# adaLN weight segments held in fours, and eight row tiles of products issued back to back

## The chip, the core and the metric

The kernel runs on one core of a Trainium2 chip. The metric is the device time of one execution in microseconds (us); lower is better. The engines that matter here are TensorE (PE in the profile, with its weight loads as PEld), VectorE (DVE), ScalarE (ACT), GpSimd (POOL) and the SyncE queue (SP), which issues nearly all weight transfers.

## The reference

One decoder layer is applied to a prompt of 256 rows and to eight samples of eight rows, 320 rows in all, with D_MODEL = 2048. Everything is float32.

```python
mod = silu(c) @ w_ada + b_ada                     # c: 9 rows, w_ada: 2048 x 12288
sh1, sc1, gt1, sh2, sc2, gt2 = split(mod, 6)
h = rmsnorm(x, g_pre_mix) * (1 + sc1) + sh1
proj = h @ w_in                                   # 2048 x 5136: q k v, z, a, b, u
o  = gated delta rule on conv(q, k, v), 8 heads, gated by silu(z)
y5 = S5 state space on u, gelu, @ w_glu, gate, norm
x = x + gt1 * rmsnorm(concat(o, y5) @ w_out, g_post_mix)
h = rmsnorm(x, g_pre_ffn) * (1 + sc2) + sh2
f = (silu(h @ w_gate) * (h @ w_up)) @ w_down      # 5632 wide
x = x + gt2 * rmsnorm(f, g_post_ffn)
```

The change is about the first line. Its nine rows of `c` (one of the prompt, eight of the samples) meet a weight matrix of 100 MB, nearly a third of all the bytes that the kernel reads.

## The kernel before, in words

**Streamed weights.** Each weight matrix comes through twelve buffers ("slots") of [128, 1024] float32, 512 KB each. A `Seg` is one such piece: `nk` row tiles of 128 rows by `ncol` columns. The list `items` holds all segments in the order in which TensorE uses them. `fetch` issues loads on the SyncE queue, in that order, as long as more than `WRES = 3` slots are free. `pump` splits a loaded segment into a high part (`whi`, a copy on ScalarE, L490) and a low part (`wlo`, a subtraction on VectorE, L491), each in a slot of its own, after which the raw slot is free again. It looks at no segment that lies `AHEAD = 4` or more places beyond the current one, and it wants three free slots. `mm3` then makes three products for every 128 x 128 block of weights, with 320 columns of activations as the moving operand.

**adaLN segments** are not split. They are used as they come, with the weights as the moving operand and the nine rows of `silu(c)`, padded to 32 columns, as the stationary one. A product thus fills 32 of the array's 128 columns. Row tile `kt` goes to column group `kt % 4`, which writes 32 of the 128 partitions of one PSUM bank (`ps_ax`); `ada_tail` copies the bank out (`adaev`), transposes it and adds up the four groups. Twenty-two blocks of 512 columns have eight segments of two row tiles each; two blocks of 384 columns have eight of two, and two of 128 columns have two of eight. A float32 product shows as two matmul instructions in the trace, so a segment of two row tiles is four of them.

**Order of the work.** `merge` interleaves the adaLN segments in proportion with the split segments of the stage: with the input projection (four slabs of 1, 3, 4 and 8 row tiles; blocks for a slab are computed during the slab before it), with the GLU, with the first half of the output projection and with the first of four blocks of the feed-forward. Two blocks stand alone, while the first sub-layer's residual is formed. The other work (convolution, S5, delta rule) is written as generators that run "in the background": after each step of `mm3` and after each segment `tick` lets them emit what an emission clock expects to be ready. All engines' streams are in order, so this clock sets where the background work stands between the streamed products. The clock charges 0.024 us for an adaLN product whose column group is not the first.

Of the kernel before, what the change touches and what calls it, by code (L numbers as in the profile page):

```python
# [79 lines left out]
class Seg:  # L80
    """One streamed [128, <=1024] piece of a weight matrix: kts row tiles by cols columns."""

    def __init__(self, src, k0, nk, c0, nc_, body, split=True):
        self.src, self.k0, self.nk, self.c0, self.ncol = src, k0, nk, c0, nc_
        self.body, self.split = body, split
        self.raw = self.hi = self.lo = None


class Paced:
    """The operations of a layer as generators, which wait until the operands are expected to be there."""  # L90
# [20 lines left out]
class Layer:  # L111
    def __init__(self, ctx, tc, I, O, stop=None):
# [12 lines left out]
        self.stage_end, self.in_bg = 0.0, False  # L125
        nc = self.nc
# [3 lines left out]
    # ---------------------------------------------------------------- emission clock  # L130
    # The instruction streams are in order, so what runs in the background is emitted where its
    # inputs are expected to be there; the clock below estimates when that is, from the engines'
    # queues and the last writes and reads of each tile.
# [15 lines left out]
    def _start(self, eng, outs, ins, same):  # L149
        """When the operands allow an operation of an engine to start."""  # L150
# [15 lines left out]
    def fits(self, eng, outs, ins):  # L166
        """Whether an operation emitted now would hardly hold up its engine."""
        c = self.clk
        t = self._start(eng, outs, ins, 0.0)
        if eng == "PE":  # L170
            return t <= c["now"] + self.EPS_PE
        return (eng == "SP" or c[eng] <= c["now"] + self.LIM) and t <= max(c[eng], c["now"]) + self.EPS
# [28 lines left out]
    def _slot(self, tile, tag, cap):  # L201
        """A new tile takes the place of the one of its tag whose last use lies furthest back."""
# [9 lines left out]
    def ready(self, *aps):  # L212
        """When these are written."""
        return max((self.rd[k][0] for ap in aps for k in self._keys(ap) if k in self.rd), default=0.0)
# [5 lines left out]
    def mbank(self, tag="mm"):  # L220
        """A PSUM bank that has been read when the streamed products get to it."""
# [7 lines left out]
    def gate(self, *ts):  # L229
        """Let the background go on until these times."""  # L230
# [75 lines left out]
    def mm(self, out, lhsT, rhs, start=True, stop=True):  # L306
# [8 lines left out]
        if not self._run("PE", c, (out,), (lhsT, rhs)):  # L315
            return
        return self.T.matmul(out, lhsT, rhs, start=start, stop=stop)  # L317

    def tr(self, out, in_, b=0):
        p = in_.shape[0]  # L320
        if not self._run("PE", 0.00086 * p, (out,), (in_,)):
# [12 lines left out]
    def take(self, tag, n=1):  # L334
        """Wait until n buffers of a tag are free; give() returns them once their last use is emitted."""
# [9 lines left out]
    def idle(self, tag):  # L345
        """PSUM banks of a tag that are free and have been read."""
# [7 lines left out]
    def bg(self, gens, k=1, front=False):  # L354
        """Run generators in the background, k of them at a time; each yield waits for what it emitted."""
# [39 lines left out]
    # ---------------------------------------------------------------- streaming  # L395
# [8 lines left out]
    def emit(self):  # L404
# [5 lines left out]
        for it in self.items:  # L410
# [10 lines left out]
            for t in (it.hi, it.lo) if it.split else (it.raw,):  # L421
                self.wput(t)
            it.raw = it.hi = it.lo = None
            self.cur += 1

    def fetch(self):
        """Load ahead, leaving room for a split and one column block of adaLN."""
# [4 lines left out]
    def pump(self, force=-1):  # L432
        """Split the segments that have arrived, as far ahead as there is room."""
# [12 lines left out]
    def ws(self, name, dt=F32):  # L446
        """The slot that has been free the longest."""
# [15 lines left out]
    def _dma(self, q, n, out=None, in_=None):  # L463
        """A transfer of n words from one of the queues."""
# [28 lines left out]
    def mm3(self, s, ps, m, act, first, last):  # L493
        """ps += W[:, chunk m].T @ act over the row tiles of s; act(kt) -> (hi, lo)."""
# [11 lines left out]
    def split_act(self, hl, src):  # L506
        """hl [128, 2, N] f32r <- hi and lo parts of src [128, N]."""
# [6 lines left out]
    # ---------------------------------------------------------------- phase 0  # L514
    def setup(self):
# [28 lines left out]
        # row vectors, one feature tile per partition: those of the first norm, and the others  # L544
# [33 lines left out]
        # silu(c), transposed, nine rows padded to 32  # L578
# [14 lines left out]
        # mean square of x, and x transposed  # L593
# [10 lines left out]
        # per-feature columns  # L604
# [17 lines left out]
    def setup_x(self):  # L622
        """Eight feature tiles of x, transposed; and the mean squares."""
# [19 lines left out]
    def setup_x2(self):  # L643
        """The other eight."""
# [11 lines left out]
    def setup_late(self):  # L656
        """The other per-feature columns; the space of the inputs goes to the mixer."""
# [25 lines left out]
    def later(self, t):  # L683
        """Hold a background stage back for t more microseconds."""
# [34 lines left out]
    # ---------------------------------------------------------------- adaLN  # L719
    def ada(self, c0, ncol):  # L720
        """Segments that leave mod[:, c0/128 .. , :] for ncol (256 or 512) columns of w_ada."""
        nk = 1024 // ncol
        st = {}

        def body(s):
            if s.k0 == 0:
# [4 lines left out]
            for kk in range(nk):  # L731
                kt = s.k0 + kk
                g = kt % 4
                self.mm(ps[32 * g:32 * g + 32, :ncol], self.cs[:, kt, :],
                        s.raw[:, kk * ncol:(kk + 1) * ncol], start=kt < 4, stop=kt >= KT - 4)
                if g == 3 and kk < nk - 1:
                    self.tick()
# [4 lines left out]
        return [Seg(self.I["w_ada"][0], k0, nk, c0, ncol, body, split=False) for k0 in range(0, KT, nk)]  # L742
# [23 lines left out]
    def modulate(self, kt, rsb, sh0, dst):  # L766
        """hi/lo of (x * rs) * A + shift for one feature tile, in place of x."""
# [36 lines left out]
    # ---------------------------------------------------------------- input projection  # L804
# [141 lines left out]
    def put(self, kind, i, ps, si):  # L946
        """Add a finished chunk to its place."""
# [39 lines left out]
    def z_gate(self, i):  # L987
        """Twice silu(z)."""
# [8 lines left out]
    # ---------------------------------------------------------------- conv  # L997
    def conv_hist(self):
        """Last rows of the conv state, transposed in front of each sample's columns."""
# [15 lines left out]
    def conv_state(self):  # L1015
        """The last rows of every sequence before the convolution, back in rows, four tiles at a time."""
# [50 lines left out]
    def expm1(self, out, x, tmp):  # L1067
        """exp(x) - 1 of a small tile: 2^k * series(x - k ln 2) + (2^k - 1)."""
# [19 lines left out]
    # ---------------------------------------------------------------- S5 tables  # L1088
    def trans(self, nm, src, hf):
        """Four tables from the transposes of src."""  # L1090
# [8 lines left out]
    def c_tables(self):  # L1099
        """Per channel tile, block diagonal over the two groups of a pair: two each of re and im of  # L1100
        [(pair, abar B or B, channel), state], then [state, (pair, channel)] of C and abar C; here C."""
# [23 lines left out]
    def s5_setup(self):  # L1125
# [49 lines left out]
        # angle in turns, reduced to half a turn either way  # L1175
# [10 lines left out]
        # sine and cosine - 1 from series at a quarter of the angle  # L1186
# [99 lines left out]
    # ---------------------------------------------------------------- S5 scan  # L1286
# [15 lines left out]
    def s5_in(self, ch):  # L1302
        """Even and odd steps of a pair's channels on top of each other, two pairs to 128 partitions."""
# [12 lines left out]
    def s5_pair(self, q):  # L1316
        """Two groups: states on the partitions, every second step held, in a rotating frame."""
# [82 lines left out]
    def s5_state_out(self):  # L1400
        """Final states back to rows of (group, state)."""
# [21 lines left out]
    # ---------------------------------------------------------------- gated delta rule  # L1423
# [1092 lines left out]
```

## Time and profile before

| | |
|---|---|
| median of 3 runs | 1903.72 us (1900.76 to 1905.53) |
| span of the profiled execution | 1904.5 us; no other time of that execution is given |
| TensorE busy | 1845.4 us (97%) |
| TensorE weight loads | 1603.9 us (84%) |
| VectorE, ScalarE, GpSimd busy | 1007.1, 771.5, 384.9 us |
| mean granted TensorE clock | 0.987 |
| read from HBM | 321.25 MB |

The span runs from the first to the last instruction. Matmuls are pipelined and their ends are modelled, so that two neighbours overlap in the record; the time that one takes from the others is read from the start of one to the start of the next. DMA share is the mean busy share of the sixteen DMA engines.

### The profile page before, as it was taken

The page shows a single profiled execution, that of the slowest core. Times are in us where ns is not written, and L with a number is a line of the kernel's source. Part 1 is how long each engine was busy: PE and PEld are TensorE (multiplying, and loading weights), DVE is VectorE, ACT ScalarE, POOL GpSimd, SP SyncE. Part 2 cuts the span into 40 slices and gives each one's busy share as a digit, 9 for nine tenths or more (in the row PEclk, how much of TensorE's full clock was granted, in tenths as well). Part 3 has the DMA queues.
Part 4 walks back from the last instruction along what each step waited for, and adds up shares of the span by engine and source line. Part 5 has one row for each costly group of instructions (what it writes and reads, how often), then busy time and mean ns, then how long its engine had stood idle before and what let it go on. Part 6 is the DMA issues. An engine that isn't in the chain of part 4 may idle for free.

```text
span 1904.5 us, 32280 instructions
## 1 busy us (share of the span) xinstructions
PE 1845.4 (97%) x12619; PEld 1603.9 (84%) x12619; DVE 1007.1 (53%) x1896; ACT 771.5 (41%) x1503; POOL 384.9 (20%) x577
## 2 busy tenths in 40 slices
PE   6899999999999989999899999999999999999998
PEld 4667787666677667789699999999999999999997
DVE  3677677878764554543833333444444334434444
ACT  3433355545564434453533333333333333333343
POOL 1003674666404211115600000000000000000043
PEclk9999999999999988999999999999999999999999
DMA  8899644555585964676565556454555545655452
GB/s 267 273 322 292 162 115 143 180 170 172 169 262 152 278 185 117 182 222 209 179 176 158 161 171 184 146 155 132 147 167 154 146 132 149 171 148 151 128 150 89
DMA packets 487953, 336.38 MB, mean 177 GB/s; under 512 B 29328, under 2 KB 439656, under 8 KB 487472
## 3 DMA queue, kind: packets, MB, share of 16 engines
q1 hardware_dynamic: 473842, 328.60, 58.3%
q10 hardware_dynamic: 13542, 5.40, 1.1%
q8 instruction: 99, 1.62, 0.4%
q14 instruction: 54, 0.43, 0.1%
q0 software_dynamic: 416, 0.32, 0.1%
HBM read 321.25 MB, written 13.02 MB: 176 GB/s over the span
## 4 chain that ended last, share of the span: by engine, by line
PE 89%; DVE 4%; DMA 3%; POOL 2%; ACT 1%; issue 1%; SPq 0%; ACTq 0%; DVEq 0%; POOLq 0%
PE ps_mm L317 43%; PE ps_bA L317 22%; PE ps_bB L317 15%; PE ps_ax L317 6%; PE ps_bB L323 1%; POOL tab L279 1%; DVE wlo L491 1%; DVE u L279 1%; PE ps_bA L323 1%; PE ps_mm L323 1%; DVE acc L279 1%; DMA x<-in_x_prompt_dram 1%; DMA braw<-in_b_im_dram 1%; DMA raw<-in_w_in_dram 0%; ACT whi L490 0%
## 5 line engine op out<-in xcount | busy, mean ns | idle before, releaser
L491 DVE TENSOR_TENSOR wlo<-raw,whi 128x1024 fp32r<-128x1024 f32 (+2 forms) x441 | 496.4, 1126 | 612.0 <-ACT whi L490 369.5
L490 ACT ACTIVATE whi<-raw 128x1024 fp32r<-128x1024 f32 (+2 forms) x441 | 424.3, 964 | 398.9 <-DVE wlo L491 289.5
L317 PE MATMUL ps_mm<-h,whi 128*128 128x320 f32 x1344 | 297.0, 308 | 0.0
L317 PE MATMUL ps_mm<-hT,whi 128*128 128x320 f32 x1204 | 289.9, 326 | 6.1 <-DVE hT L279 3.7
L317 PEld LDWEIGHTS ps_mm<-hT,whi 128*128 128x128 f32 x1204 | 198.2, 191 | 54.9 <-issue 32.1
L317 PEld LDWEIGHTS ps_mm<-h,whi 128*128 128x128 f32 x1344 | 224.4, 187 | 4.2 <-ACT gs L262 1.7
L317 PE MATMUL ps_mm<-h,wlo 128*128 128x320 f32 x672 | 206.6, 307 | 0.0
L317 PE MATMUL ps_mm<-hT,wlo 128*128 128x320 f32 x602 | 187.5, 311 | 0.0
L279 POOL TENSOR_TENSOR sqa<-acc 128x320 f32<-128x320 f32 x1 | 0.7, 722 | 863.3 <-DVE acc L279 863.3
L317 PE MATMUL ps_bA<-h,whi 128*128 128x320 f32 x736 | 163.8, 310 | 1.5 <-ACT whi L490 1.5
L317 PE MATMUL ps_bB<-h,whi 128*128 128x320 f32 x736 | 162.7, 308 | 0.0
L317 PE MATMUL ps_mm<-f,whi 128*128 128x320 f32 x704 | 155.7, 309 | 0.0
L317 PE MATMUL ps_ax<-raw,cs 128*32 128x512 f32 (+2 forms) x832 | 152.1, 583 | 0.0
L317 PEld LDWEIGHTS ps_bA<-h,whi 128*128 128x128 f32 x736 | 123.9, 189 | 3.4 <-ACT whi L490 2.4
L317 PEld LDWEIGHTS ps_mm<-h,wlo 128*128 128x128 f32 x672 | 125.9, 187 | 0.0
L317 PEld LDWEIGHTS ps_bB<-h,whi 128*128 128x128 f32 x736 | 122.9, 187 | 3.4 <-issue 3.4
L317 PEld LDWEIGHTS ps_mm<-f,whi 128*128 128x128 f32 x704 | 117.6, 188 | 2.5 <-ACT acc L262 1.7
L317 PEld LDWEIGHTS ps_mm<-hT,wlo 128*128 128x128 f32 x602 | 114.7, 191 | 0.0
L317 PE MATMUL ps_bA<-h,wlo 128*128 128x320 f32 x368 | 113.7, 309 | 0.9 <-DVE wlo L491 0.9
L317 PE MATMUL ps_bB<-h,wlo 128*128 128x320 f32 x368 | 113.2, 308 | 0.0
L317 PE MATMUL ps_mm<-f,wlo 128*128 128x320 f32 x352 | 108.5, 308 | 0.0
L279 POOL TENSOR_TENSOR AB<-AB 128x169 f32<-128x169 f32 x128 | 83.9, 681 | 28.2 <-DVE AB L279 18.1
(579 smaller groups left out, 3043.0 us busy)
## 6 DMA issues: line engine op xcount, KB each, us to landing
raw<-in_w_ada_dram SPq DMA_DIRECT2D x180, 512.0 KB
raw<-in_w_gate_dram SPq DMA_DIRECT2D x88, 512.0 KB
raw<-in_w_up_dram SPq DMA_DIRECT2D x88, 512.0 KB
raw<-in_w_in_dram SPq DMA_DIRECT2D x66, 512.0 KB
raw<-in_w_down_dram SPq DMA_DIRECT2D x64, 512.0 KB
raw<-in_w_out_dram SPq DMA_DIRECT2D x32, 512.0 KB
raw<-in_w_down_dram SPq DMA_DIRECT2D x64, 192.0 KB
raw<-in_w_glu_dram SPq DMA_DIRECT2D x16, 512.0 KB
```

The lines of the kernel that those rows point to most:

```text
L279: return e.tensor_tensor(out, a, b, op=op)
L317: return self.T.matmul(out, lhsT, rhs, start=start, stop=stop)
L323: return self.T.transpose(out, in_, self.ident[b:b + p, b:b + p])
L490: return (self.S.activation(s.hi[:, :w], s.raw[:, :w], AF.Copy), self.V.tensor_tensor(s.lo[:, :w], s.raw[:, :w], s.hi[:, :w].bitcast(F32), ...
L491: self.V.tensor_tensor(s.lo[:, :w], s.raw[:, :w], s.hi[:, :w].bitcast(F32), op=OP.subtract))
```

## The change

A segment of adaLN weights now has a flag `hold`. It is set where the segment does not complete a multiple of eight row tiles. A held segment's body only puts it on a list, and its slot is kept. The segment that completes eight row tiles issues the products of all that were held: 16 matmul instructions in a row for 512 columns, over the column groups 0, 1, 2, 3, 0, 1, 2, 3. Then the slots are given back. `merge` keeps the segments of such a set of eight row tiles together in the stream, where before other segments could stand between them. The emission clock gets a charge of 0.095 us whenever the shape of the array's tiles changes (`retile`). The call to `tick` between groups of four is gone. The comments and docstrings that the diff also removes are left out here.

```diff
-    def __init__(self, src, k0, nk, c0, nc_, body, split=True):
+    def __init__(self, src, k0, nk, c0, nc_, body, split=True, hold=False):
...
-        if not self._run("PE", c, (out,), (lhsT, rhs)):
+        if not self._run("PE", c + self.retile(lhsT), (out,), (lhsT, rhs)):
...
+    def retile(self, lhsT):
+
+        k = tuple(32 if n <= 32 else 64 if n <= 64 else 128 for n in (lhsT.shape[0], self._n(lhsT)))
+        t = 0.0 if k == self.tiling else 0.095
+        if not self.dry:
+            self.tiling = k
+        return t
...
             it.body(it)
-            for t in (it.hi, it.lo) if it.split else (it.raw,):
-                self.wput(t)
-            it.raw = it.hi = it.lo = None
+            if not it.hold:
+                for t in (it.hi, it.lo) if it.split else (it.raw,):
+                    self.wput(t)
+                it.raw = it.hi = it.lo = None
             self.cur += 1
...
         nk = 1024 // ncol
-        st = {}
+        st = {"held": []}
 
         def body(s):
-            if s.k0 == 0:
+            st["held"].append(s)
+            if s.hold:
+                return
+            if s.k0 + nk <= self.ADA_KT:
                 self.await_(lambda: not self.ada_busy)
                 self.ada_busy = True
                 st["ps"] = self.bank("ax")
             ps = st["ps"]
-            for kk in range(nk):
-                kt = s.k0 + kk
-                g = kt % 4
-                self.mm(ps[32 * g:32 * g + 32, :ncol], self.cs[:, kt, :],
-                        s.raw[:, kk * ncol:(kk + 1) * ncol], start=kt < 4, stop=kt >= KT - 4)
-                if g == 3 and kk < nk - 1:
-                    self.tick()
+            for x in st["held"]:
+                for kk in range(nk):
+                    kt = x.k0 + kk
+                    g = kt % 4
+                    self.mm(ps[32 * g:32 * g + 32, :ncol], self.cs[:, kt, :],
+                            x.raw[:, kk * ncol:(kk + 1) * ncol], start=kt < 4, stop=kt >= KT - 4)
+            for x in st["held"]:
+                if x is not s:
+                    self.wput(x.raw)
+                    x.raw = None
+            st["held"] = []
             if s.k0 + nk == KT:
                 self.bg(self.ada_tail(ps, c0, ncol), front=True)
             self.tick()
 
-        return [Seg(self.I["w_ada"][0], k0, nk, c0, ncol, body, split=False) for k0 in range(0, KT, nk)]
+        return [Seg(self.I["w_ada"][0], k0, nk, c0, ncol, body, split=False, hold=(k0 + nk) % self.ADA_KT > 0)
+                for k0 in range(0, KT, nk)]
+
+    ADA_KT = 8
...
         if j * len(a) < i * len(b) and j < len(b) or i >= len(a):
+            while b[j].hold:
+                out.append(b[j])
+                j += 1
             out.append(b[j])
             j += 1
```

## Rows read from the trace of the kernel before

**Rows 1.** The page: busy time of each engine, and the chain's shares.

```profile
PE 1845.4 (97%) x12619; PEld 1603.9 (84%) x12619; DVE 1007.1 (53%) x1896; ACT 771.5 (41%) x1503; POOL 384.9 (20%) x577
...
PE 89%; DVE 4%; DMA 3%; POOL 2%; ACT 1%; issue 1%; SPq 0%; ACTq 0%; DVEq 0%; POOLq 0%
```

**Rows 2.** Busy time by stage: window, length, engines' busy us, PEclk, DMA share, GB/s.

```profile
76.00:160.00 84.00, 81.57 (x536) 57.52 (x536) 62.91 (x230) 25.70 (x53) 0.00 (x0) 0.99 0.93 304
160.00:220.00 60.00, 56.42 (x440) 44.69 (x440) 35.75 (x84) 20.58 (x47) 34.09 (x55) 1.00 0.79 227
...
320.00:560.00 240.00, 238.85 (x1385) 161.30 (x1385) 188.76 (x347) 126.91 (x357) 116.75 (x158) 1.00 0.60 182
...
620.00:700.00 80.00, 76.90 (x762) 53.33 (x760) 44.72 (x119) 34.26 (x63) 17.76 (x23) 0.96 0.93 267
700.00:845.00 145.00, 138.43 (x1152) 108.88 (x1153) 74.23 (x189) 69.14 (x195) 15.52 (x30) 0.93 0.55 159
...
935.00:1175.00 240.00, 240.00 (x1574) 223.38 (x1573) 97.62 (x124) 87.14 (x129) 10.46 (x22) 1.00 0.59 167
```

**Rows 3.** The same windows, instructions that write or read `ps_ax` alone.

```profile
38.00:76.00 38.00, 6.61 (x64) 1.88 (x64) 0.00 (x0) 0.96 (x2) 0.93 0.85 287
...
76.00:160.00 84.00, 23.79 (x144) 3.49 (x144) 0.00 (x0) 2.39 (x4) 0.99 0.93 304
160.00:220.00 60.00, 10.53 (x48) 1.48 (x48) 0.00 (x0) 1.18 (x2) 1.00 0.79 227
...
320.00:560.00 240.00, 38.30 (x192) 6.15 (x192) 0.00 (x0) 3.59 (x6) 1.00 0.60 182
560.00:700.00 140.00, 26.40 (x128) 3.69 (x128) 0.00 (x0) 2.39 (x4) 0.98 0.79 230
700.00:845.00 145.00, 16.83 (x64) 2.30 (x64) 0.00 (x0) 1.18 (x2) 0.93 0.55 159
845.00:935.00 90.00, 8.73 (x64) 1.79 (x64) 0.00 (x0) 1.17 (x2) 0.96 0.65 200
935.00:1175.00 240.00, 16.83 (x64) 2.30 (x64) 0.00 (x0) 1.18 (x2) 1.00 0.59 167
```

**Rows 4.** Timeline: bursts of 4, 8 and 32 adaLN instructions (start, length in us).

```profile
1122.43 0.46 PE L317 MATMUL ps_bB<-f,whi 128*128 128x320 f32 x2
...
1122.72 0.31 PE L317 MATMUL ps_bB<-f,wlo 128*128 128x320 f32 x1
...
1122.96 1.05 PE L317 MATMUL ps_ax<-raw,cs 128*32 128x512 f32 x4
...
1123.94 0.56 PE L317 MATMUL ps_bB<-f,whi 128*128 128x320 f32 x2
...
563.22 1.07 PE L317 MATMUL ps_ax<-raw,cs 128*32 128x512 f32 x8
...
923.13 3.64 PE L317 MATMUL ps_ax<-raw,cs 128*32 128x512 f32 x32
```

**Rows 5.** Waits of the SyncE queue: us in total, times, longest us.

```profile
SPq L461 <- PE ps_mm L317: 529.9, 203, 9.8
```

**Rows 6.** Tile `raw`: the two halves of a split, ns min/median/max.

```profile
L490 ACT ACTIVATE whi<-raw x441: 310/1052/1087, 24.9 to 1870.0; 128x1024 fp32r<-128x1024 f32 x119, 128x384 fp32r<-128x384 f32 x21, 128x768 fp32r<-128x768 f32 x7
L491 DVE TENSOR_TENSOR wlo<-raw,whi x441: 293/1225/1981, 26.0 to 1871.3; 128x1024 fp32r<-128x1024 f32 x119, 128x384 fp32r<-128x384 f32 x21, 128x768 fp32r<-128x768 f32 x7
```

**Rows 7.** DMA at its busiest, columns as in rows 2.

```profile
136.00:156.00 20.00, 19.91 (x139) 15.35 (x136) 15.76 (x64) 5.48 (x8) 0.00 (x0) 1.00 0.99 330
```

**Rows 8.** Tile `u`: the last S5 read-out, and its split into GLU inputs.

```profile
L262 ACT ACTIVATE hT<-u x16: 236/337/436, 523.6 to 555.8; 128x256 fp32r<-128x256 f32 x8, 128x64 fp32r<-128x64 f32 x8
...
L304 DVE SCALAR_TENSOR_TENSOR u<-u,gv,ps_bA x1: 562/562/562, 516.3 to 516.3; 128x336 f32<-128x336 f32 x1
```

**Rows 9.** VectorE timeline at the delta rule's end; tile `hz`, the projection's second half.

```profile
829.80 0.48 DVE L304 SCALAR_TENSOR_TENSOR z<-ps_bA,gv,z 128x256 f32<-128x256 f32 x1 [1.40 <-PE ps_bA L323]
...
843.47 0.48 DVE L279 TENSOR_TENSOR hz<-z,hz 128x320 fp32r<-128x320 f32 x1
...
L317 PE MATMUL ps_mm<-hz,whi x256: 307/308/392, 842.4 to 898.5; 128*128 128x320 f32 x128
L262 ACT ACTIVATE hz<-z x8: 455/457/464, 832.0 to 838.0; 128x320 fp32r<-128x320 f32 x8
```

More of the change, by code (lines that the diff above doesn't have):

```diff
@@ L80 @@
 class Seg:
-    def __init__(self, src, k0, nk, c0, nc_, body, split=True):
+    def __init__(self, src, k0, nk, c0, nc_, body, split=True, hold=False):
         self.src, self.k0, self.nk, self.c0, self.ncol = src, k0, nk, c0, nc_
-        self.body, self.split = body, split
+        self.body, self.split, self.hold = body, split, hold
         self.raw = self.hi = self.lo = None
@@ L125, in __init__ @@
         self.stage_end, self.in_bg = 0.0, False
+        self.tiling = (128, 128)
         nc = self.nc
@@ L314, in mm @@
             c = max(0.11, 0.0017 * n)
-        if not self._run("PE", c, (out,), (lhsT, rhs)):
+        if not self._run("PE", c + self.retile(lhsT), (out,), (lhsT, rhs)):
             return
         return self.T.matmul(out, lhsT, rhs, start=start, stop=stop)
+    def retile(self, lhsT):
[4 more added lines that the diff above has]
+        return t
     def tr(self, out, in_, b=0):
         p = in_.shape[0]
-        if not self._run("PE", 0.00086 * p, (out,), (in_,)):
+        if not self._run("PE", 0.00086 * p + self.retile(in_), (out,), (in_,)):
             return
```

## The prediction

> **What bounds the kernel now.** I read the page first, then the busy times by stage, then the adaLN products alone, then who waits for whom. The page shows TensorE busy for 97% of the span and on 89% of the chain that ended last [rows 1], so what is taken off TensorE should come off the time, unless the stage then finds another limit. The table by stage says where it may. From 935 to 1175 us TensorE has no gap at all and the transfers take 0.59 of the DMA engines; from 320 to 560 us it is the same with VectorE at 189 of 240 us. But from 76 to 160 us and from 620 to 700 us the DMA engines stand at 0.93 beside a full TensorE, so there two limits lie close together, and from 700 to 845 us TensorE is not quite full and its granted clock sinks to a mean of 0.93 of 2.4 GHz [rows 2].
>
> **The price of the adaLN products, before and after.** The 512-column segments are 704 instructions, 44 sets of 16. The `ps_ax` table gives their busy time by stage: 23.8 us for 9 sets (76 to 160), 10.5 for 3 (160 to 220), 38.3 for 12 (320 to 560), 26.4 for 8 (560 to 700), 16.8 for 4 (700 to 845), 8.7 for 4 (845 to 935) and 16.8 for 4 (935 to 1175) [rows 3]. The bursts show why it is so much. A burst of 4 instructions (one segment, two column groups) takes 1.05 us, one of 8 (four groups) 1.07 us: the second pair of groups is all but free. The one burst of 32 takes 3.64 us, so each further 8 cost (3.64 - 1.07) / 3 = 0.86 us. Is the busy time the true price? The burst of 4 at 1122.96 begins 0.24 us after the product ahead of it, where products of this kind follow each other after 0.145 us (1122.43 to 1122.72 is two of them), and the next product starts 0.98 us after the burst did. Entry 0.095 plus 0.98 makes 1.07, so 1.05 will serve, and the entry gap needs no term of its own [rows 4].
>
> After the change a set of 16 is one burst of two fours: 1.07 + 0.86 = 1.93 us. Stage by stage: 9 x 1.93 = 17.4, saved 6.4; 3 x 1.93 = 5.8, saved 4.7; 12 x 1.93 = 23.2, saved 15.1; 8 x 1.93 = 15.4, saved 11.0; 4 x 1.93 = 7.7, saved 9.1, 1.0 and 9.1 in the last three. The gross sum is 56.4 us. It is a little high: between 320 and 560 us some bursts are mixed with S5 products that run inside them, and their time counts twice. The 384-column sets before 76 us I put at nothing: 64 instructions take 6.6 us in long bursts already, under a DMA share of 0.85 [rows 3].
>
> A rule of the Trainium skill speaks against four column groups being free: "TensorE: Matmul & The Clock Gate", section "Measured speedup vs the span model", lists 2.38 times for three column tiles, not three times. Three passes at once would then take 3 / 2.38 = 1.26 of one. If a four took 1.26 times what a pair does, the 88 fours would cost some 88 x 0.26 x 0.9 = 21 us more (an estimate from that page and the 0.9 us of a four), and the gross sum would be 36. The trace does not agree (1.07 against 1.05), and I keep the trace's.
>
> **What holding costs.** Loads are paced by slots: the SyncE queue's waits at the load line are for TensorE to release a buffer, 529.9 us in 203 waits for `ps_mm` products alone [rows 5]. A held set keeps four of the twelve. Counted through the code for a stage with two split segments per set: when the set's turn comes, its four slots, two for the next segment's halves, four raw segments and two free ones make twelve, so about one set and two split segments are under way ahead of TensorE. The loads are not starved, I think. The split is tighter. `AHEAD = 4` is filled by the set's own four segments, so the first split segment behind a set is split only once the segment ahead of the set has been issued, and its `wlo` takes a slot that this segment has just left. It has the 1.93 us of the set as cover. `whi` takes 1.05 us and `wlo` 1.23 [rows 6]; if `whi` ran before, the cover is enough by 0.7 us; if ScalarE still has a read of that segment's PSUM bank ahead of it, `whi` starts late and some 0.4 to 0.9 us of TensorE lie open. Bounds for one set: nothing, and the whole 2.28 us. I take 0.3 us on the mean, since the half that needs the fresh slot is the second. Behind the waiting product are all of TensorE's later products, background too.
>
> **Stage by stage, what arrives.** 76 to 160: 0.93 of the DMA engines at 304 GB/s; the best stretch inside had 0.99 at 330 [rows 7]. The bytes stay, so the stage can shrink by at most 84 x (1 - 304/330) = 6.6 us and probably little; I take 1.5 (0 to 6.4). 160 to 220: 3 of 4.7, since it starts with what the transfers left behind. 320 to 560: 15.1 less the double count (1.5, my estimate) less 12 x 0.3 is 10; I take 11, because S5 sets no limit: its last read-out is at 516.3, 40 us ahead of the stage's end, and the splits up to 555.8 that follow wait for buffers which this stage gives back [rows 8].
>
> 560 to 845 has 20.1 us gross, and here I expect to lose most. The second half of the output projection starts at 842.4 and needs all eight heads. The last head's gated output is written at 829.8 and the last `hz` half at 843.5, one product column ahead of its use [rows 9]. `hz` itself is 8 x 0.46 us on ScalarE and one 0.48 on VectorE behind, so it could be done at 835. The slack of the delta rule is thus 842.4 - 835 = 7 us; past that, a shorter stream only makes TensorE wait for heads. The delta rule's own chain gains a little from fewer bursts in its way. I take 9 (bounds 5 and 20). Its start moves with the stream, so what was saved earlier is kept.
>
> 845 to 935: nothing; TensorE waits there for the residual. 935 to 1175: no other work is near; 9.1 less 4 x 0.3 is 8.
>
> The better emission clock (0.095 us at each change of shape, and no more segments that it thinks nearly free) moves background work by fractions of a microsecond either way. It removes no wait that the trace shows; I put it at nothing, with 5 us both ways in the range. Removed `tick` calls: nothing, since every product of a split segment still has one.
>
> Sum: 1.5 + 3 + 11 + 9 + 8 = 32.5 us. The span is 1904.5, 0.8 above the median; taken from the median, 1903.7 - 32.5 = 1871 us.
>
> **The rivals.** (a) Everything arrives: 1903.7 - 56.4 = 1847, or 1850 with the double count. For it: TensorE at 97%. Against: the heads at 843.5 and the two stages at 0.93.
>
> (b) Only the stages without a second limit gain: 8 from the feed-forward, 6 from 320 to 560 with VectorE at 79% in the way, 1 each from the others: 1903.7 - 17 = 1887. For it: the stages of [rows 2] and the late heads.
>
> (c) It does not do what it says, or what it gives is eaten: fours don't run together, or losses at the sets come to the gain. The burst of 32 speaks against the first. About 1900.
>
> (d) Slower: the first segment behind a set is split only after the set. Place: every set, on TensorE, before a `whi` product. Price: 2.28 us x 44 = 100 us at the worst, against 56 gained, so 1903.7 + 44 = 1948. It decides from 56.4 / 44 = 1.28 us a set. For it: VectorE and ScalarE already wait in turn on each other and on slots. Against: the code emits that split ahead of the set. The Trainium skill has a rule on this side, "Perfetto Trace Analysis", section "Optimization Strategy": the same gap repeating on the engine that should be full can mean too few buffers for the next tile. The trace of before shows no such gap in 935 to 1175 us; with four slots held it could.
>
> **How the numbers follow.** Forecast (1860 to 1882): 0.48. (a), under 1860: 0.17. (b), 1882 to 1898: 0.21. (c): 0.07. (d): 0.07. The range reaches into (a) down to 1850 and through most of (b) up to 1893; about 0.08 lies below and 0.14 above. Within 0.3% is 5.7 us, about what a measurement of this kernel can tell from no change: faster 0.86, same 0.07, slower 0.07.
>
> **What would show it.** Bursts of 16 of about 1.93 us, 44 of them, `ps_ax` busy near 8 us instead of 16.8 in the feed-forward. That stage shorter by 8 us, with no gap behind its four sets. Loads from 76 to 160 us at a higher GB/s and the stage hardly shorter. A gap or a lower granted clock on TensorE just ahead of the first `hz` product. Wrong would be: gaps of over a microsecond behind each set (d), or bursts of 16 well over 2 us (c), or the delta rule ending earlier by as much as the stream is shorter (a).

## The result, and the profile after

The changed kernel takes 1883.84 us (median of 4 runs, 1876.16 to 1884.37) against 1903.93 us of the kernel before on the same chip (4 runs too): a ratio of 0.9888, 95% interval 0.9868 to 0.9908. That is 20 us off, where 32.5 were forecast. The profiled execution has a span of 1881.8 us at a mean granted clock of 0.976 of 2.4 GHz (before: 1904.5 us at 0.987).

The page of the changed kernel: busy time, the chain, and the group of adaLN products.

```profile
PE 1804.8 (96%) x12619; PEld 1615.8 (86%) x12619; DVE 1007.1 (54%) x1896; ACT 770.9 (41%) x1501; POOL 378.2 (20%) x577
...
PE 59%; DVE 2%; ACT 1%; DMA 0%; POOL 0%; issue 0%; SPq 0%; POOLq 0%; DVEq 0%
...
L318 PE MATMUL ps_ax<-raw,cs 128*32 128x512 f32 (+2 forms) x832 | 95.7, 576 | 1.1 <-DMA raw<-in_w_ada_dram 1.1
```

TensorE is busy for 40.6 us less than in [rows 1], and the span is 22.7 us shorter. So some 18 us that the bursts gave back went into time in which TensorE has nothing to do. The chain of this page could be followed back only to 717 us (its shares add up to 62%), so it can't be set beside the chain of [rows 1]. The adaLN products alone by stage, in windows that follow the stages as they lie now (columns as in [rows 2]):

```profile
67.00:155.00 88.00, 17.31 (x144) 3.76 (x144) 0.00 (x0) 2.39 (x4) 0.96 0.96 320
155.00:255.00 100.00, 5.77 (x48) 1.25 (x48) 0.00 (x0) 1.16 (x2) 0.95 0.65 182
255.00:561.00 306.00, 23.62 (x192) 5.33 (x192) 0.00 (x0) 3.47 (x6) 0.98 0.59 170
561.00:727.00 166.00, 15.39 (x128) 3.34 (x128) 0.00 (x0) 2.35 (x4) 0.95 0.67 199
727.00:829.00 102.00, 7.70 (x64) 1.67 (x64) 0.00 (x0) 1.17 (x2) 0.90 0.71 210
829.00:916.00 87.00, 7.49 (x64) 1.76 (x64) 0.00 (x0) 1.19 (x2) 0.98 0.61 189
916.00:1161.00 245.00, 7.70 (x64) 1.67 (x64) 0.00 (x0) 1.18 (x2) 0.99 0.62 176
```

The instruction counts are those of [rows 3]; the busy times fall by 6.5, 4.8, 14.7, 11.0, 9.1, 1.2 and 9.1 us, 56.4 in all, as forecast. A set in the feed-forward, in TensorE's timeline:

```profile
991.47 0.30 PE L318 MATMUL ps_mm<-h,wlo 128*128 128x320 f32 x1
991.71 1.92 PE L318 MATMUL ps_ax<-raw,cs 128*32 128x512 f32 x16
993.56 0.56 PE L318 MATMUL ps_bB<-h,whi 128*128 128x320 f32 x2
993.95 0.31 PE L318 MATMUL ps_bB<-h,wlo 128*128 128x320 f32 x1
```

Sixteen instructions, 1.85 us to the next product, and 0.24 us from the product ahead, of which 0.145 are that product's own. A set costs 1.95 us of TensorE.

What each stage made of it is read from the first product of each stage in the timeline (a stage runs to the first product of the next):

| stage | begins before, after | length before, after | difference | forecast |
|---|---|---|---|---|
| second slab | 70.2, 66.8 | 93.0, 87.8 | -5.2 | -1.5 |
| third slab | 163.2, 154.6 | 106.2, 100.8 | -5.5 | -3 |
| fourth slab, with S5 and convolution | 269.4, 255.3 | 289.0, 305.4 | +16.4 | -11 |
| GLU | 558.4, 560.7 | 136.5, 166.7 | +30.2 | -9, with the next |
| output projection, first half | 694.9, 727.4 | 147.5, 101.1 | -46.4 | |
| second half, and residual | 842.4, 828.5 | 85.9, 87.3 | +1.4 | 0 |
| first feed-forward block | 928.3, 915.8 | 255.5, 245.4 | -10.1 | -8 |

The three stages in the middle change by +16.4, +30.2 and -46.4 us, but together they take 573.0 us before and 573.2 after. There 34.8 us of busy time went from the adaLN products and nothing arrived. The start up to the second slab is 3.4 us shorter as well, which no term of the forecast names.

Added up from start to start of TensorE's instructions (so that the entry of 0.095 us counts with the product ahead of a burst), the adaLN products of this middle stretch take 30.0 us less (76.2 to 46.2), the split segments' products 19.4 more (294.2 to 313.6) and the background's 11.1 more (202.4 to 213.5). Three things stand behind the 30 us. The first is in TensorE's waits over the whole span (what it waited for, us in total, times, longest):

```profile
PE ps_bB L318 <- POOL bx L280: 10.4, 5, 4.6
PE ps_mm L318 <- DVE wlo L501: 7.6, 13, 1.4
...
PE ps_bA L318 <- DVE kr L298: 2.6, 5, 0.8
...
PE ps_mm L318 <- ACT whi L500: 2.0, 3, 1.3
```

The largest of them, for `bx` (a step of S5 on GpSimd, 2.4 us before), lies in the third slab and not in the middle. The same view of before has no line for `ps_mm` on `whi` or `wlo`. Two of these places, all engines' lines of the timeline that matter:

```profile
388.21 1.06 ACT L500 ACTIVATE whi<-raw 128x1024 fp32r<-128x1024 f32 x1 [1.35 <-issue]
...
388.65 1.92 PE L318 MATMUL ps_ax<-raw,cs 128*32 128x512 f32 x16
...
392.14 0.56 PE L318 MATMUL ps_mm<-hx,whi 128*128 128x320 f32 x2
...
392.27 3.23 DVE L501 TENSOR_TENSOR wlo<-raw,whi 128x1024 fp32r<-128x1024 f32 x2
...
394.07 0.42 PE L318 MATMUL ps_mm<-hx,wlo 128*128 128x320 f32 x1 [1.38 <-DVE wlo L501]
```

```profile
780.29 0.44 ACT L263 ACTIVATE u<-ps_mm 128x320 f32<-128x320 f32 x1 [1.12 <-PE ps_mm L318]
780.63 2.00 ACT L500 ACTIVATE whi<-raw 128x1024 fp32r<-128x1024 f32 x2
...
781.71 2.36 DVE L501 TENSOR_TENSOR wlo<-raw,whi 128x1024 fp32r<-128x1024 f32 x2 [1.17 <-ACT whi L500]
...
782.99 0.42 PE L318 MATMUL ps_mm<-hT,wlo 128*128 128x320 f32 x1 [0.38 <-DVE wlo L501]
```

In the first place two `whi` products run behind the set, and the third product waits 1.38 us for `wlo`: its `whi` was begun at 388.21, but VectorE comes to `wlo` only at 392.27, behind convolution and S5 work. In the second VectorE stands ready and waits for `whi`, which ScalarE begins at 780.63, just behind its read of a PSUM bank of the projection. In the middle stretch there are 12 such waits, behind 9 of the 24 sets, three of the first kind and nine of the second. TensorE is idle in them for 8.6 us (6.6 and 2.0 in the view of that stretch alone); from start to start of the products they take 10.2 us, or 0.43 us a set over all 24.

The second is the clock. Five-microsecond windows over the end of the GLU (busy us of PE, PEld, DVE, ACT, POOL, then PEclk, DMA share, GB/s):

```profile
710.00:715.00 5.00, 3.12 (x33) 1.95 (x31) 2.03 (x7) 4.65 (x17) 0.00 (x0) 1.00 0.21 62
715.00:720.00 5.00, 3.40 (x20) 2.47 (x19) 3.67 (x11) 3.37 (x14) 1.18 (x2) 0.74 0.01 3
720.00:725.00 5.00, 4.64 (x17) 3.70 (x16) 3.89 (x9) 1.82 (x5) 1.61 (x3) 0.50 0.01 2
725.00:730.00 5.00, 5.00 (x17) 3.54 (x16) 2.98 (x9) 1.30 (x3) 1.03 (x2) 0.50 0.18 52
...
735.00:740.00 5.00, 5.00 (x18) 3.83 (x18) 2.41 (x8) 2.10 (x7) 0.00 (x0) 0.50 0.44 151
740.00:745.00 5.00, 5.00 (x34) 3.75 (x37) 1.27 (x5) 3.61 (x14) 0.00 (x0) 0.87 0.04 2
```

In TensorE's timeline the last streamed product of the GLU and the first of the output projection:

```profile
706.67 0.46 PE L318 MATMUL ps_mm<-hT,whi 128*128 128x320 f32 x2
706.96 0.31 PE L318 MATMUL ps_mm<-hT,wlo 128*128 128x320 f32 x1
...
727.43 0.88 PE L318 MATMUL ps_mm<-hT,whi 128*128 128x320 f32 x2
```

For 20 us no streamed product runs: the projection needs the normed S5 branch, whose first tile VectorE begins at 716.3 us, and behind that it comes after delta-rule steps that stand ahead of it in TensorE's stream. Those are small products with steps on VectorE and ScalarE between them. TensorE is busy for 3.1 and 3.4 us of five, then the granted clock falls to 0.50 (1.2 GHz) and stays there for 24 us, 15 of them with TensorE busy throughout. In all, the middle stretch has 51 us at half clock, before 27.

The third is in the waits of the middle stretch again: TensorE's idle time ahead of background products is 18 us there, before 11 (added up from that view without its lines for `ps_mm` on `whi` and `wlo`). It lies in many short waits; the most, 2.6 us, are for `kr`, a delta-rule step on VectorE.

### The profile page after: what moved, and what is told of

The parts are those of the page before. It is cut to its first block, busy times and chain, and to the rows that moved or that the text cites. A ratio compares the mean times of both kernels' runs of the same rounds, so it can differ in the third digit from the quotient of the medians.

```text
span 1881.8 us, 32310 instructions
## 1 busy us (share of the span) xinstructions
PE 1804.8 (96%) x12619; PEld 1615.8 (86%) x12619; DVE 1007.1 (54%) x1896; ACT 770.9 (41%) x1501; POOL 378.2 (20%) x577
## 4 chain that ended last, share of the span: by engine, by line
PE 59%; DVE 2%; ACT 1%; DMA 0%; POOL 0%; issue 0%; SPq 0%; POOLq 0%; DVEq 0%
PE ps_mm L318 30%; PE ps_bA L318 14%; PE ps_bB L318 13%; DVE acc L280 1%; PE ps_ax L318 1%; DVE u L280 1%; DVE wlo L501 0%; ACT whi L500 0%; PE ps_bA L332 0%; DMA S<-in_state_delta_dram 0%; POOL h2t L280 0%; ACT rs L263 0%; PE ps_mm L332 0%; ACT ch L263 0%; ACT yo L263 0%
## 5 line engine op out<-in xcount | busy, mean ns | idle before, releaser
L318 PEld LDWEIGHTS ps_mm<-hT,whi 128*128 128x128 f32 x1204 | 203.1, 194 | 29.2 <-issue 19.7
L318 PE MATMUL ps_ax<-raw,cs 128*32 128x512 f32 (+2 forms) x832 | 95.7, 576 | 1.1 <-DMA raw<-in_w_ada_dram 1.1
```

## The experiments

All versions were timed beside the kernel before on their chip (1900.7 to 1905.6 us); ratios are to it.

### Is it the emission clock, or the bursts?

**The clock alone** (kernel before, with the charge for changes of shape in both kinds of TensorE instruction, products and transposes, as the changed kernel has it):

```diff
-        if not self._run("PE", c, (out,), (lhsT, rhs)):
+        if not self._run("PE", c + self.retile(lhsT), (out,), (lhsT, rhs)):
...
-        if not self._run("PE", 0.00086 * p, (out,), (in_,)):
+        if not self._run("PE", 0.00086 * p + self.retile(in_), (out,), (in_,)):
```

> The kernel before with the new emission clock alone (0.095 us charged at each change of array shape), no holding. Theory A (what the change lost between the input projection's last slab and the output projection's second half was lost to the first split segment behind each set, 10.2 us of gaps ahead of wlo products there): about 1904, within 4 us of the kernel before. Theory B (the clock now puts background work earlier in the stream, so that the delta rule overtakes the GLU and TensorE runs cold): 1914 to 1924.

Measured: 1948.46 us (1947.71 to 1952.24), ratio 1.0239, 1.0221 to 1.0257. A loss of 46 us, outside both expectations: 21 in the third slab (127.2 us) and 21 in the middle (594.4). What theory B describes is there (the last `hz` half is written at 796.4 us, 88 ahead of its first use, and the middle has 51 us at half clock), but the loss is more than twice as large, and half of it lies in a slab. Its waits of TensorE show the kind:

```profile
PE ps_bA L318 <- DVE si L280: 10.1, 2, 8.9
PE ps_mm L318 <- ACT hT L263: 8.2, 7, 3.0
```

With more charged, the clock takes more background work for ready and puts it ahead of streamed products; where it isn't ready, TensorE stands, once for 8.9 us.

**The changed kernel with a charge of nothing, and with half of it:**

```diff
-        t = 0.0 if k == self.tiling else 0.095
+        t = 0.0
```

The second version has `0.05` in place of `0.095`.

> The changed kernel with the charge for a change of shape set to nothing; holding and bursts of 16 stay. Theory A: 1884, within 4 us. Theory B: 1864 to 1874, with the delta rule ending near the start of the output projection's second half again.

> The changed kernel (held), charge for a change of shape 0.05 us. Theory H: 1880 to 1888, as at 0 and at 0.095. Theory S: from 1866 to 1900.

Measured: 1884.29 us (0.9901, 0.9875 to 0.9928) without it and 1888.66 (0.9926, 0.9903 to 0.9949) with half, against 1883.84. That is theory A's time, and theory H's within a microsecond. Beside held sets the charge changes the time by 5 us at most; the price that it has alone can't be added to anything. Yet without the charge the GLU and the projection's first half take 137.5 and 141.4 us, nearly as before, and the last `hz` half is written at 822.7 us, 3 ahead of its use, as theory B said. So it was the charge that moved these two stages by +30 and -46 us, and undoing the move gained nothing clear.

### Does holding cost what it keeps?

**Sets kept together in the stream, but nothing held**: each segment issues its own products and gives its slot back at once, with no background work between them.

```diff
-            if not it.hold:
-                for t in (it.hi, it.lo) if it.split else (it.raw,):
-                    self.wput(t)
-                it.raw = it.hi = it.lo = None
+            for t in (it.hi, it.lo) if it.split else (it.raw,):
+                self.wput(t)
+            it.raw = it.hi = it.lo = None
...
-            self.tick()
+            if not s.hold:
+                self.tick()
```

> The four segments of a set still stand together in the stream, but none is held: each issues its products when its turn comes and gives its slot back, with no background call between them. If holding the slots is what costs, this is faster than the changed kernel by 5 us or more, with the same bursts of 16. If only the order of the segments counts, it is the same within 4 us, 1880 to 1888, since the next split is as late.

Measured: 1867.71 us (0.9811, 0.9790 to 0.9832), 16 us faster than the changed kernel (15 by the two ratios). Its adaLN products in the second slab and in the first feed-forward block:

```profile
67.00:155.00 88.00, 17.31 (x144) 3.76 (x144) 0.00 (x0) 2.40 (x4) 1.00 0.98 329
...
898.00:1145.00 247.00, 7.70 (x64) 1.67 (x64) 0.00 (x0) 1.16 (x2) 0.99 0.60 173
```

They are the same to the hundredth: the bursts come from the neighbourhood in the stream alone. But its waits show the gaps too:

```profile
PE ps_mm L318 <- DVE wlo L500: 8.9, 13, 1.8
```

So the time is the one expected if holding costs, but holding isn't what makes the split late. What the 16 us are was asked with the other charges, nothing and half:

> Set kept together but not held, charge for a change of shape 0. Theory H (holding the slots is what costs the 16 us between the changed kernel and the same sets not held): 1866 to 1872, about 16 us under the held kernel with this charge (1884.3). Theory S (the three kernels differ by where the emission clock happens to set the background work): anywhere from 1866 to 1890, and the difference held less not held changes by more than 8 us from one charge to the next.

> Set kept together but not held, charge for a change of shape 0.05 us. Theory H: 1866 to 1872. Theory S: anywhere from 1866 to 1890.

| median, us | charge 0 | 0.05 | 0.095 |
|---|---|---|---|
| eights held | 1884.3 | 1888.7 | 1883.8 |
| eights together, not held | 1884.6 (1879 to 1887) | 1873.4 (1871 to 1879) | 1867.7 (1865 to 1870) |

The price of holding is -0.3, 15.3 or 16.1 us, depending on the charge (-1, 13 and 15 by the ratios). A price of four kept buffers alone would be there in every column. It isn't, and the charge changes nothing but where the clock puts the background work: theory S, and both times without holding miss theory H's range. Whether a smaller price of holding hides under these differences the six times can't tell.

### Are the gaps behind the sets what the middle lost?

**A longer look ahead for splits**, and, more narrowly, **a look ahead that does not count held segments**:

```diff
-    AHEAD, WRES = 4, 3
+    AHEAD, WRES = 8, 3
```

```diff
-        while self.ns < min(self.cur + self.AHEAD, self.nl):
+        while self.ns < self.nl:
+            held = sum(1 for x in self.segs[self.cur:self.ns] if x.hold)
+            if self.ns - held >= self.cur + self.AHEAD:
+                break
```

> The changed kernel with AHEAD = 8 instead of 4, so that the segment behind a set may be split one segment earlier. Theory A: the gaps ahead of wlo products behind sets (10.2 us in 12 places from 255 to 828 us) go, 1872 to 1876. Theory B: 1884, within 4 us.

> The changed kernel, but held segments do not count in the split window of AHEAD = 4, so the first split segment behind a set is split a whole segment earlier; elsewhere the window is as before. Theory A (gaps ahead of wlo products behind sets are lost time): those gaps, 10.2 us from 255 to 828 us, go, 1872 to 1877. Theory S: the gaps go as well, but the time moves by any amount up to 20 us either way, as it did with AHEAD = 8.

Measured: 1906.69 us (1.0017, 0.9994 to 1.0040) and 1906.2 (10 runs from 1894 to 1917; 1.0016, 0.9989 to 1.0043). Theory A is refuted by both, and the second is 22 us slower than the changed kernel, just beyond theory S. With `AHEAD = 8` two gaps are left behind sets in the middle, 1.0 us of idle time instead of 8.6, and the kernel is 23 us slower. Its waits, and the delta rule's end:

```profile
PE ps_bA L318 <- DVE kr L298: 6.7, 4, 5.2
...
PE ps_mm L318 <- DVE wlo L501: 2.1, 6, 0.7
```

```profile
L318 PE MATMUL ps_mm<-hz,whi x256: 304/308/636, 858.4 to 916.6; 128*128 128x320 f32 x128
...
L280 DVE TENSOR_TENSOR hz<-z,hz x8: 483/488/489, 858.8 to 861.6; 128x320 fp32r<-128x320 f32 x8
```

The first `hz` product starts at 858.4, and VectorE's halves of `hz` are written from 858.8 to 861.6, while the products already run: the projection waits for the delta rule. It is so in the narrower version too (840.3, and 840.7 to 843.5), and both have the wait of 5.2 us for `kr`, a step of the delta rule on VectorE. That splits issued earlier stand ahead of the delta rule's steps there is my reading; no run had the one without the other.

By stage most of what the two traces lose lies ahead of the middle, though (the first is of an execution 8 us above its median, the second of one 9 us below):

| longer than in the changed kernel, us | up to the second slab | third slab | the three middle stages | second half | span |
|---|---|---|---|---|---|
| `AHEAD = 8` | 8.6 | 13.6 | 7.6 | 2.2 | 31.5 |
| held segments not counted | 5.0 | 6.6 | 0.2 | 2.4 | 14.0 |

The gaps behind sets can be taken away, but in these two versions the middle didn't get shorter by it, and the stages ahead of it got longer. In the third slab they have 27 and 14 us at half clock, where the changed kernel has 10; why wasn't taken apart.

### Is the middle bound by TensorE's work?

**Three of four products left out** in the column blocks from 4096 to 10240, in the changed kernel and in the kernel before; all loads stay:

```diff
+                    mid = 4096 <= c0 < 10240
+                    if mid and kt < KT - 4:
+                        continue
...
-                            x.raw[:, kk * ncol:(kk + 1) * ncol], start=kt < 4, stop=kt >= KT - 4)
+                            x.raw[:, kk * ncol:(kk + 1) * ncol], start=mid or kt < 4, stop=kt >= KT - 4)
```

> The changed kernel, but of the twelve adaLN blocks of columns 4096 to 10240 (those between the last slab and the output projection's second half) only the products of the last four row tiles are made; loads, holding and order stay. So those outputs are not the layer's. It takes some 46 - 12 x 1.07 = 33 us of TensorE work out of that stretch. Theory P (the stretch is bound by TensorE's work, and the change's gain there was eaten by gaps behind the sets): 1849 to 1856. Theory C (the chain of background work, S5 and then the delta rule, bounds the stretch, so that freed TensorE time is not worth its length): 1872 or more.

> The kernel before with the same products left out (kept: the last four row tiles of the blocks of columns 4096 to 10240, as two bursts of 4 a block). It takes some 76 - 24 x 1.07 = 50 us of TensorE work out of the stretch. Theory P: 1850 to 1858. Theory C: 1885 or more, with the last hz half written at or behind the start of the projection's second half.

Measured: 1868.33 us (0.9832, 0.9803 to 0.9862) and 1881.83 (0.9894, 0.9864 to 0.9925). Both lie between the two theories' ranges. From start to start the adaLN products of the middle take 34 us less (46.2 to 12.1) and 56 less (76.2 to 19.9). 16 and some 20 arrive in the median total, and of the three middle stages 573.2 became 562.5, 573.0 became 561.9. The trace of the second is of its slowest execution (1894.5 us, 13 above the median). So a microsecond taken off TensorE there is worth 0.2 to 0.3 by the traces, and 0.3 to 0.5 by the medians. The rest is seen in the same account. In the changed kernel the split segments' products take 24 us more: TensorE's idle time ahead of them rose from 8.6 to 24.0 us, and their time at half clock by some 13. In the kernel before the background takes 40 us more, since 65 us of it now run at half clock where 17 did. The sign of theory C, a last `hz` half at or behind the start of the second half, did not come: it is written 4 us ahead in the kernel before, 31 us ahead in the changed one.

These shares are of two particular versions. A product that is left out isn't charged to the emission clock either, so the background moved as well: in the kernel before the GLU went from 136.5 to 117.4 us and the projection's first half from 147.5 to 181.3. No run took TensorE's work out and kept the order.

### Smaller sets

**Sets of four row tiles**, two segments, held as in the changed kernel; and the same sets kept together without holding (the edit of above):

```diff
-            if s.k0 + nk <= self.ADA_KT:
+            if s.k0 + nk <= max(nk, self.ADA_KT):
...
-    ADA_KT = 8
+    ADA_KT = 4
```

> The changed kernel with sets of four row tiles: two segments held together, bursts of 8 instructions. TensorE pays 44 x (2 x 1.09 - 1.95) = 10 us more than with bursts of 16, but the split window of four reaches past a set, and a set keeps two slots instead of four. If the gaps behind sets and the slots are what was lost, they go: 1876 to 1884, as fast as the changed kernel or faster. If not: 1890 to 1898.

> Sets of four row tiles (two segments) kept together, each segment's products issued as it comes, its slot given back at once, no tick between them. Against held sets of four (1865.3 us) only the holding is gone. Theory A: what sets of eight lose is the place that a set takes among the four segments that may be split ahead, so with sets of two nothing is left that holding could cost: 1860 to 1871, and the stretch from the fourth slab to the projection's second half within 8 us of the 550.6 of the held fours. Theory B: the slots that a set keeps cost time by themselves, as the 16 us between eights held and not held suggested; a set of four keeps two of twelve, so half of that should come back: 1853 to 1860. Theory C: the differences between such versions are only where the background work happens to fall: any value from 1855 to 1885.

Measured: 1865.32 us (0.9814, 0.9785 to 0.9842) held, 1868.97 (0.9802, 0.9783 to 0.9820) not held: the same. The first is faster than either range given for it; the second is theory A's time, though theory C's wide range holds it too. Two bursts of 8 cost TensorE 0.23 us more than one of 16, 10 us over all sets, and yet both are 15 to 19 us faster than the changed kernel (14 to 16 by the ratios). The held fours, three lines of TensorE's waits and the delta rule's end:

```profile
PE ps_bA L318 <- ACT whi L500: 3.4, 2, 1.8
PE ps_bA L318 <- DVE wlo L501: 2.6, 4, 0.7
...
PE ps_bB L318 <- DVE kr L298: 0.9, 1, 0.9
```

```profile
L318 PE MATMUL ps_mm<-hz,whi x256: 304/308/310, 808.6 to 864.6; 128*128 128x320 f32 x128
...
L280 DVE TENSOR_TENSOR hz<-z,hz x8: 482/484/486, 760.9 to 765.6; 128x320 fp32r<-128x320 f32 x8
```

No wait of `ps_mm` products for `wlo` or `whi` is left (the `ps_bA` ones are in all versions), the time at half clock in the middle is 24 us where the changed kernel has 51, and the delta rule is done 43 us early. The middle is 550.6 us, 22.6 less than in the changed kernel; not held it is 554.0. A set of two segments leaves two of the four places of the look ahead to the split segments behind it. That the whole gain is from this isn't shown: the eights that aren't held reach the same total with their gaps, by a shorter second and third slab (85.0 and 93.9 us, where the held fours take 86.7 and 103.3).

## Why the prediction came out as it did

**The price of a set: right.** 1.93 us forecast, 1.85 and an entry of 0.095 measured, and 56.4 us of busy time gone. The dearer price that was estimated from the Trainium skill ("TensorE: Matmul & The Clock Gate", "Measured speedup vs the span model", 2.38 times for three column tiles) isn't seen: eight instructions over four groups take 1.00 us here (the held fours), and four over two groups took 0.98 [rows 4]. No run has one group alone, so the table's own number isn't tested.

**The slabs: 4.5 us forecast, 10.7 measured.** The term for the second slab was mis-sized. I took 1.5 of at most 6.6 us since the transfers were at 0.93; the stage gained 5.2, nearly as much as TensorE's busy time in it (89.2 to 83.4 us), and over the whole stage the transfers went from 293 GB/s at a share of 0.91 to 319 at 0.96. Not held, they reached 329 GB/s. A share of 0.93 beside a full TensorE was still a stage that followed TensorE's work.

**The middle: 20 us forecast (11 and 9), nothing measured.** This is the step that failed. Two reasons given for it were wrong.

- For 320 to 560 us I argued that S5 sets no limit, and so that TensorE's saving arrives. But the stretch wasn't bound by TensorE's work, though TensorE was busy for 238.9 of 240 us [rows 2]: with three of four products left out, a fifth to a half arrives, in the kernel before as well, and the rest becomes waiting for splits or time at half clock (with the background in another order, as said above). A TensorE that is busy all the time in a stretch where background work fills the places between shows that work was found for it, not that it sets the end.
- For 560 to 845 us I named the delta rule's slack of 7 us as the limit. In the changed kernel its last `hz` half is written at 786.3 us, 42 ahead of the projection's second half at 828.5; in [rows 9] it was one column ahead. The clock's charge put background work earlier; the GLU became longer by it and the projection's first half shorter, for without the charge both are nearly as before. The limit is real (with a longer look ahead the second half starts on halves that are still being written), but it isn't a fixed date.

What took the 30 us there: 10.2 us of gaps behind sets and about 13 us of half clock (46 more split products at twice 0.145 us, 6.7 us, and half of the 13.2 us by which the background's time at half clock grew). The remaining 7 are about what TensorE's idle time ahead of background products grew by (11 to 18 us). The three overlap a little, so the sum is no more than an estimate. That the gaps and the half clock, and not something else, are what has to go is supported by the held fours, whose middle is 22.6 us shorter without the gaps and with 24 us at half clock; it isn't proved, since the longer look ahead removed the gaps and didn't shorten the middle.

**What holding costs: the mechanism right, the cause only in part.** 0.3 us a set was taken, 0.43 measured in the middle. The trace shows it nearly as told in nine of the 12 waits: `whi` begins late on ScalarE, and `wlo` follows it. Sometimes it is the read of a PSUM bank that was named (780.29), elsewhere other ScalarE work. In the other three VectorE is late, behind other work, which the prediction didn't name. The Trainium skill's rule ("Perfetto Trace Analysis", "Optimization Strategy") that a gap which repeats on the engine that should be full can mean too few buffers fits its look, but not its cause: sets that aren't held have 13 such waits as well. With the same twelve buffers and a longer look ahead the idle time in them goes from 8.6 to 1.0 us. It is the four places of the look ahead, which a set of eight fills, held or not, and a set of four doesn't.

**The clock: nothing was taken, with 5 us both ways.** Between both kernels as they are that holds (1884.3 without the charge, 1883.8 with it), but the reason given, that it moves work by fractions of a microsecond, is wrong: alone it costs 46 us, with sets that aren't held it is worth 17, and beside held sets it moves the end of the GLU by tens of microseconds. The removed `tick` calls, put at nothing too, were not tried by themselves.

**The feed-forward: 8 us forecast, 10.1 measured**, one gap of 0.39 us behind its four sets. The step with nothing else near was the one that came out.

So the time lies within the range as a whole (1850 to 1893 us), 2 us outside the forecast's own part and in that of rival (b), and it does so by errors in both directions: the middle gave 20 us less than forecast, the slabs 6 more, the feed-forward 2 more, and the start 3.4 that no term had. That the total came no further out is luck. Rival (b) is the better account in its idea, that only stages without a second limit gain, but it booked 6 us for 320 to 560, where nothing came, and 1 for each slab, where 5 came. Rival (d) showed its sign, at a fifth of its worst price. The sign named for rival (a), a delta rule that ends earlier by as much as the stream is shorter, came as well (57 us earlier, 843.5 to 786.3), though (a) was wrong: most of that is the charge, without which it ends at 822.7.

What stays open: which placement of the background work makes the 15 to 20 us between versions whose bursts are the same. Holding, the charge and the look ahead each move it, and no run fixed that order while changing one of them.

## What to carry to other kernels

To run column groups of the array together it is enough that their products are neighbours in the stream: keeping the buffers back is not needed (the bursts were the same, 17.31 us in both), and a set that leaves room in the look ahead for what follows it did better here, by 15 to 19 us. Before a saving on a busy engine is booked in a stretch filled with other work, leave the work out there and see what share arrives; here it was 0.2 to 0.5, against 1.1 in a stretch with nothing else; and see whether that moves the other work too. A better cost in a planner's clock is a change of its own, and can lose more (46 us) than the edit that it comes with gains.

## What the runs showed of the hardware

Four column groups run side by side at almost no loss against two. A burst of 8 by itself takes 1.00 us to the next product in the held fours, where a burst of 4 took 0.98 before [rows 4]; in a burst of 16 each 8 take 0.93.

```profile
1004.83 1.06 PE L318 MATMUL ps_ax<-raw,cs 128*32 128x512 f32 x8
1005.83 0.56 PE L318 MATMUL ps_bB<-h,whi 128*128 128x320 f32 x2
```

The granted clock stayed at half for long after TensorE was full again: in the changed kernel it was busy for 5.00 of 5 us from 725 to 740 us, with 17 or 18 instructions in each 5 us, and had 0.50 throughout. In the held fours the hole ahead was deeper (busy for 1.89 of 5 us), and the fall short:

```profile
720.00:725.00 5.00, 1.89 (x9) 0.97 (x8) 4.08 (x14) 3.66 (x13) 0.00 (x0) 0.81 0.69 194
725.00:730.00 5.00, 4.63 (x29) 2.93 (x30) 2.95 (x7) 4.75 (x19) 1.43 (x2) 0.50 0.81 211
730.00:735.00 5.00, 5.00 (x30) 3.83 (x30) 4.95 (x16) 2.56 (x10) 1.18 (x2) 1.00 0.02 5
```

What makes the difference no run here tells.
